# RMS norms of a hybrid decoder step: last squares summed by TensorE, and 1/rms spread as a stationary operand

## Chip, core and metric
One core of one Trainium2 chip runs the kernel. The metric is the time of one execution on the device, in microseconds (us). Three executions of the kernel before gave 2889.6, 2897.57 and 2901.08 us; the median is 2897.57.

## The reference, cut to what matters
One inference step of a decoder with two layers, for a prompt of 1024 tokens and 8 sample tokens. Five RMS norms lie on the way: one ahead of each mixer, one ahead of each MLP, one at the end.

```
def _rmsnorm(x, g):
    y = x * rsqrt(mean(x * x, axis=-1, keepdims=True) + 1e-6)
    return y * g
# layer 0 and layer 1:
h = _rmsnorm(x, norm_mix[layer]);  x = x + mixer(h) ...
h = _rmsnorm(x, norm_mlp[layer]);  x = x + square(relu(h @ w_up)) @ w_down
out = _rmsnorm(x, norm_final)
```

Everything is float32. The kernel splits each float32 operand of the large products into two parts (`h` and `l`, tiles `xh`/`xl`, `uh`/`ul`, `ih`/`il`, `wh`/`wl`) and multiplies three times; the products inside the norm are plain float32 products.

## The kernel before, in words
**Layout.** Activations stand transposed: 1024 features in 8 chunks (`KC`) of 128 partitions, tokens along the free axis. The tokens are cut in two halves, `u = 0` with 512 tokens and `u = 1` with 520 (512 and the 8 samples). `half()` is the output projection and MLP of one layer and one half; the attention and recurrence stages run beside it.

**The norm.** The gain of the norm is multiplied into the split activations before a projection (`gain`), and the factor 1/rms of a token is multiplied into the projection's result. So the projections need not wait for the norm, but the first eviction of their results from PSUM does. The factor is made in four steps:

1. `sumsq` (lines 251 to 262) is called once for each feature chunk `n`. ScalarE squares the chunk (L257 for the first, L260 for the others), VectorE adds the square to the running sum `sq` (L261). In `finish`, the last stage, the same is written out (L1608, L1611, L1612, tiles `fsq` and `fst`).
2. `rms` (lines 264 to 287) adds the 128 partitions: for each 128 tokens (`c`) one product with the 128x128 piece of `sq` as stationary operand and a column of ones as moving operand (L271), which puts the sums of 128 tokens on 128 partitions, one column for each `c`.
3. VectorE divides by 1024 and adds epsilon (L274, L276), GpSimd takes the power -0.5 (L279), into `v` (tile `rv`), which it has set to 1.0 before (L273).
4. The factor is spread over all partitions: for each `c`, VectorE multiplies the identity with a column of `v` (L284, the diagonal `rd`, two buffers), TensorE multiplies it with a full matrix of ones as stationary operand (L285), and ScalarE copies the result to `rb` (L287).

**The eleven calls of rms.** By their row sums on TensorE they lie in the profiled execution at: 1 and 2, the first norm, both halves, at 35 and 39 us (4 and 5 products of 128 tokens); 3, MLP of layer 0, first half, 501 (4); 4, mixer of layer 1, first half, 1050 (4); 5, MLP of layer 0, second half, 1261 (5); 6, mixer of layer 1, second half, 1697 (5); 7, MLP of layer 1, first half, 1929 (4); 8, final norm, first half, 2442 (4); 9, MLP of layer 1, second half, 2512 (5); 10 and 11, final norm, second half, in two blocks of 256 and 264 tokens, at 2870 and 2882 (2 and 3). These are 45 products at L271 and 45 at L285.

**Order.** The program text gives instructions a priority and a queue; a scheduler with a simulated timeline then fixes the order of each engine's queue, among what is ready at that simulated time. Engines work their queues in order. The waits for buffers come from pools of tiles: a tile of a tag with `bufs` buffers waits until the tile that had the buffer has been read for the last time. `half()` is a generator whose pieces are put between the attention stages as filler work for TensorE (`tick`, `fill`); calls 3, 5 and 7 lie in such stretches. Call 8 has no filler left: the second half of layer 1 can begin only after its stage has ended.

**Weights.** `wsplit` loads a block of weights, ScalarE makes `wh` (L117) and GpSimd makes `wl` (L118); GpSimd's queue holds these and the norm's power and memsets.

Of the kernel before, what the change touches and what calls it, by code (L numbers as in the profile page):

```python
# [10 lines left out]
F32 = mybir.dt.float32  # L11
# [3 lines left out]
AF = mybir.ActivationFunctionType  # L15
ALU = mybir.AluOpType
# [6 lines left out]
HW = (NP // 2, T - NP // 2)  # L23
HS = (slice(0, HW[0]), slice(HW[0], T))
PW = (512, 640)
BLOCKS = (((0, 512),), ((0, 256), (256, 264)))
KC = D // 128
# [37 lines left out]
class Step:  # L65
# [98 lines left out]
    def project_rms(self, ps, src, evict, rms, us=(0, 1), w=None):  # L164

        h, l = w or self.wsplit(src, KC)
        pts = []
        for u in us:
            for o, n in BLOCKS[u]:
                pts.append((ps.tile([128, 512], F32, name="acc", tag="acc"), u, o, n))  # L170
                self.mm3(pts[-1][0][:, :n], h, l, self.ih[u], self.il[u], range(KC), slice(o, o + n))
        for u in us:
            rms(u)
        for pt, u, o, n in pts:
            evict(pt[:, :n], u, o, n)
# [75 lines left out]
    def sumsq(self, pool, x, n, sq=None, tags=(("sq", 1), ("ld", 2)), first=None):  # L251

        nc = self.nc
        w = x.shape[1]
        if n == 0:
            sq = (first or pool).tile([128, w if first is None else -(-w // 128) * 128], F32, name="sq", tag=tags[0][0], bufs=tags[0][1])
            nc.scalar.activation(sq[:, :w], x, AF.Square)  # L257
        else:
            t = pool.tile([128, w], F32, name="sqt", tag=tags[1][0], bufs=tags[1][1])
            nc.scalar.activation(t[:, :w], x, AF.Square)  # L260
            nc.vector.tensor_tensor(sq[:, :w], sq[:, :w], t[:, :w], op=ALU.add)  # L261
        return sq

    def rms(self, pool, ps, sq, rb, n):

        nc = self.nc
        full, rest = divmod(n, 128)
        cs = [(c, min(128, n - 128 * c)) for c in range(full + (rest > 0))]
        pt = ps.tile([128, 512], F32, name="acc", tag="acc")
        for c, w in cs:  # L270
            nc.tensor.matmul(pt[:w, c:c + 1], lhsT=sq[:, 128 * c:128 * c + w], rhs=self.ones[:, 0:1], start=True, stop=True)  # L271
        v = pool.tile([128, 9], F32, name="rv", tag="rv")
        nc.gpsimd.memset(v[:], 1.0)  # L273
        nc.vector.tensor_scalar(v[:, :full], pt[:, :full], 1.0 / D, EPS, op0=ALU.mult, op1=ALU.add)  # L274
        if rest:
            nc.vector.tensor_scalar(v[:rest, full:full + 1], pt[:rest, full:full + 1], 1.0 / D, EPS, op0=ALU.mult, op1=ALU.add)  # L276
        h = pool.tile([128, 9], F32, name="rp", tag="rp")
        nc.gpsimd.memset(h[:], -0.5)
        nc.gpsimd.tensor_tensor(v[:, :len(cs)], v[:, :len(cs)], h[:, :len(cs)], op=ALU.pow)  # L279
        for g in range(0, len(cs), 4):  # L280
            pt = ps.tile([128, 512], F32, name="acc", tag="acc")
            for c, w in cs[g:g + 4]:
                d = pool.tile([128, 128], F32, name="rd", tag="rd", bufs=2)
                nc.vector.tensor_scalar(d[:, :w], self.ident[:, :w], v[:, c:c + 1], None, op0=ALU.mult)  # L284
                nc.tensor.matmul(pt[:, 128 * (c - g):128 * (c - g) + w], lhsT=self.ones[:], rhs=d[:, :w], start=True, stop=True)  # L285
            w = min(512, n - 128 * g)
            nc.scalar.copy(rb[:, 128 * g:128 * g + w], pt[:, :w])  # L287

# [20 lines left out]
    def hgrn_gates(self, ph, ps, pr, first, sq):  # L309

        nc, I = self.nc, self.I
        self.fS, self.gS = ([self.dr.tile([4, 128, HW[u]], F32, name=f"{n}{u}") for u in range(2)] for n in ("fS", "gS"))
        lbp = self.col[:, C_LB:C_LB + 12].rearrange("p (h j) -> p h j", j=3)
        lb = self.cp.tile([128, 4], F32, name="lb")
        oml = self.cp.tile([128, 4], F32, name="oml")
        e = ph.tile([128, 4, 3], F32, name="lbe", tag="lbe")
        s = ph.tile([128, 4], F32, name="lbs", tag="lbs")
        nc.vector.tensor_reduce(s[:], lbp, axis=AX.X, op=ALU.max)
        nc.vector.tensor_tensor(e[:], lbp, s[:].unsqueeze(2).to_broadcast([128, 4, 3]), op=ALU.subtract)
        nc.scalar.activation(e[:], e[:], AF.Exp)  # L320
        nc.vector.tensor_reduce(s[:], e[:], axis=AX.X, op=ALU.add)
        nc.vector.reciprocal(s[:], s[:])
        nc.vector.tensor_tensor(lb[:], e[:, :, 0], s[:], op=ALU.mult)
        nc.vector.tensor_scalar(oml[:], lb[:], -1.0, 1.0, op0=ALU.mult, op1=ALU.add)
        for h in range(4):
            z = ph.tile([128, T], F32, name="z", tag="z", bufs=2)
            ev = self.scaled(z, (0, 1))
            if h:
                self.now(self.project(ps, I["w_in_e"][16 + h], ev))
            else:  # L330
                self.project_rms(ps, None, ev, lambda u: self.rms(ph, pr, sq[:, HS[u]], self.rb[u], HW[u]), w=first)
            g = ph.tile([128, T], F32, name="sg", tag="z2", bufs=2)
            nc.scalar.activation(g[:], z[:], AF.Sigmoid)
            nc.vector.tensor_scalar(g[:], g[:], oml[:, h:h + 1], lb[:, h:h + 1], op0=ALU.mult, op1=ALU.add)
            for u in range(2):
                nc.sync.dma_start(self.fS[u][h], g[:, HS[u]])
        for h in range(4):
            z = ph.tile([128, T], F32, name="z", tag="z", bufs=2)
            self.now(self.project(ps, I["w_in_e"][24 + h], self.scaled(z, (0, 1))))
            g = ph.tile([128, T], F32, name="sg", tag="z2", bufs=2)  # L340
            last = nc.scalar.activation(g[:], z[:], AF.Sigmoid)
            nc.gpsimd.tensor_tensor(g[:], g[:], z[:], op=ALU.mult)
            for u in range(2):
                nc.sync.dma_start(self.gS[u][h], g[:, HS[u]])

        self.zero = self.cp.tile([128, 1], F32, name="zero")
        nc.vector.tensor_scalar(self.zero[:], g[:, 0:1], 0.0, 0.0, op0=ALU.min, op1=ALU.max)
        self.ln_exp(last)
# [1151 lines left out]
    def half(self, layer, u, ps, pr, tp=None):  # L1500
# [40 lines left out]
        if not alone:  # L1541
            yield 1
            rms()
# [48 lines left out]
    def finish(self, mp, ps, pr, u, xs, uh, ul, wd):  # L1592

        nc, I, O = self.nc, self.I, self.O
        for n in range(2, 4):
            wd.append(self.down_parts(mp, n))
        rb = self.rb[u]
        for i, (o, m) in enumerate(BLOCKS[u]):
            sl = slice(o, o + m)
            sq = mp.tile([128, 512], F32, name="fsq", tag="t", bufs=2)  # L1600
            for n in range(KC):
                pt = ps.tile([128, 512], F32, name="acc", tag="acc")
                h, l = (w[:, 4 * (n % 2):4 * (n % 2) + 4, :] for w in wd[n // 2])
                self.mm3(pt[:, :m], h, l, uh, ul, range(4), sl)
                x = xs[n][:, sl]
                nc.vector.tensor_tensor(x, pt[:, :m], x, op=ALU.add)  # L1606
                if n == 0:
                    nc.scalar.activation(sq[:, :m], x, AF.Square)  # L1608
                else:
                    t = mp.tile([128, 512], F32, name="fst", tag="u", bufs=2)  # L1610
                    nc.scalar.activation(t[:, :m], x, AF.Square)  # L1611
                    nc.vector.tensor_tensor(sq[:, :m], sq[:, :m], t[:, :m], op=ALU.add)  # L1612
            with self.tc.high_priority():
                self.rms(mp, pr, sq, rb[:, sl], m)
            last = i == len(BLOCKS[u]) - 1
            for n in range(KC):
                x = xs[n][:, sl]
                g = self.col[:, C_FIN + n:C_FIN + n + 1]
                if n % 3 == 1 if last else n % 2:
                    nc.scalar.activation(x, x, AF.Copy, scale=g)  # L1620
                    nc.gpsimd.tensor_tensor(x, x, rb[:, sl], op=ALU.mult)
                else:
                    nc.vector.scalar_tensor_tensor(x, x, g, rb[:, sl], op0=ALU.mult, op1=ALU.mult)  # L1623
                nc.sync.dma_start(O["y"][:, n, HS[u].start + o:HS[u].start + o + m], x)
# [280 lines left out]
```

## Time and profile before

| | before |
|---|---|
| time, median of 3 | 2897.57 us |
| the profiled execution's own time | 2897.19 us |
| its span, first to last instruction | 2895.4 us |
| TensorE matmul (PE) busy | 2748.0 us, 95%, 17404 instructions |
| TensorE weight load (PEld) busy | 2449.9 us, 85% |
| VectorE (DVE) busy | 1377.6 us, 48% |
| GpSimd (POOL) busy | 1142.3 us, 39% |
| ScalarE (ACT) busy | 1038.9 us, 36% |
| mean granted TensorE clock | 0.973 of full speed |

PE and PEld are the two parts of TensorE: a weight load overlaps with the matmul before it. L12 is line 12 of the kernel. In a row of the timeline the text in square brackets is the time that the engine was idle ahead of it, and what ended that. Busy times of matmuls include a modelled end, so the spacing of a run of them says more than the length of one. SP issues the DMAs.

### The profile page before, as it was taken

How to read it: one execution, taken by the hardware profiler on the slowest of the kernel's cores; microseconds unless marked ns; L12 is line 12 of the kernel's file. 1: busy time of each engine (PE TensorE's matmuls, PEld its weight loads, DVE VectorE, ACT ScalarE, POOL GpSimd, SP SyncE). 2: the span in 40 equal slices, each digit the busy share in tenths (PEclk: the TensorE clock that was granted, in tenths of full speed). 3: DMA queues.
4: the chain of work that ended last, by engine and by line, in shares of the span. 5: the costliest groups of instructions: out<-in, count | busy, mean ns of one | idle time of the engine just before them, and what ended most of it. 6: DMA issues, size and time to landing. Idle time of an engine off the chain costs nothing. (4 is left out here: it accounts for less than half of the span.)

```text
span 2895.4 us, 44560 instructions
## 1 busy us (share of the span) xinstructions
PE 2748.0 (95%) x17404; PEld 2449.9 (85%) x17406; DVE 1377.6 (48%) x2666; ACT 1038.9 (36%) x1741; POOL 1142.3 (39%) x689
## 2 busy tenths in 40 slices
PE   8999997989989999999999989989999998999998
PEld 6999886777878878889999979968877776999997
DVE  5134378666664363474322255366544434523234
ACT  4111365552222232463232332155543222423233
POOL 2323323323764434423334435743323343344443
PEclk9999998999999999999999999999999998999999
DMA  4332454224545444423322244643235333322222
GB/s 143 107 125 75 152 163 127 89 83 154 159 115 164 132 163 147 154 88 104 121 95 88 91 158 147 222 128 93 77 110 163 110 107 126 110 89 95 90 94 74
DMA packets 174684, 349.72 MB, mean 121 GB/s; under 512 B 28914, under 2 KB 67298, under 8 KB 174474
## 3 DMA queue, kind: packets, MB, share of 16 engines
q1 hardware_dynamic: 174250, 346.81, 37.0%
q8 instruction: 137, 2.24, 0.3%
q0 software_dynamic: 224, 0.07, 0.2%
q14 instruction: 73, 0.60, 0.1%
HBM read 297.92 MB, written 48.88 MB: 120 GB/s over the span
## 5 line engine op out<-in xcount | busy, mean ns | idle before, releaser
L118 POOL TENSOR_TENSOR wl<-wr,wh 128x1024 fp32r<-128x1024 f32 (+1 forms) x361 | 866.2, 2400 | 1336.0 <-ACT wh L117 1293.1
L117 ACT ACTIVATE wh<-wr 128x1024 fp32r<-128x1024 f32 (+1 forms) x361 | 381.7, 1058 | 1088.1 <-PE acc L151 875.0
L151 PE MATMUL acc<-xh,wh 128*128 128x264 f32 (+2 forms) x2208 | 715.0, 325 | 18.1 <-DVE x L1522 8.0
L151 PE MATMUL acc<-xl,wh 128*128 128x264 f32 (+2 forms) x2208 | 711.3, 323 | 3.1 <-DVE xl L249 3.1
L151 PE MATMUL acc<-xh,wl 128*128 128x264 f32 (+2 forms) x2208 | 709.9, 322 | 0.0
L151 PE MATMUL acc<-uh,wh 128*128 128x512 f32 (+2 forms) x1856 | 607.4, 331 | 21.7 <-DVE x L1522 13.2
L151 PE MATMUL acc<-ul,wh 128*128 128x512 f32 (+2 forms) x1856 | 599.6, 324 | 6.9 <-DVE ul L1489 5.6
L151 PE MATMUL acc<-uh,wl 128*128 128x512 f32 (+2 forms) x1856 | 597.6, 323 | 0.0
L151 PEld LDWEIGHTS acc<-xh,wh 128*128 128x128 f32 x2208 | 420.3, 191 | 51.5 <-issue 10.5
L151 PEld LDWEIGHTS acc<-xl,wh 128*128 128x128 f32 x2208 | 420.7, 191 | 35.6 <-DVE xl L249 4.3
L151 PEld LDWEIGHTS acc<-xh,wl 128*128 128x128 f32 x2208 | 420.0, 190 | 29.4 <-issue 1.2
L1522 DVE TENSOR_TENSOR x<-acc,x 128x256 f32<-128x256 f32 (+1 forms) x464 | 238.3, 517 | 379.0 <-PE acc L151 376.9
L151 PEld LDWEIGHTS acc<-uh,wh 128*128 128x128 f32 x1856 | 353.0, 192 | 56.7 <-DVE x L1522 17.0
L151 PEld LDWEIGHTS acc<-ul,wh 128*128 128x128 f32 x1856 | 354.2, 191 | 33.6 <-DVE ul L1489 7.6
L151 PEld LDWEIGHTS acc<-uh,wl 128*128 128x128 f32 x1856 | 353.8, 191 | 26.8 <-issue 0.4
L1495 DVE SCALAR_TENSOR_TENSOR acc<-acc,rb 128x256 f32<-128x256 f32 (+2 forms) x192 | 100.2, 524 | 242.4 <-PE acc L151 237.7
L151 PE MATMUL acc<-ih,wh 128*128 128x512 f32 (+3 forms) x600 | 193.0, 322 | 7.3 <-ACT wh L117 4.7
L151 PE MATMUL acc<-ih,wl 128*128 128x512 f32 (+3 forms) x600 | 192.2, 323 | 6.5 <-POOL wl L118 6.5
L151 PE MATMUL acc<-il,wh 128*128 128x512 f32 (+3 forms) x600 | 192.2, 321 | 0.0
L225 DVE TENSOR_TENSOR z<-acc,rb 128x512 f32<-128x512 f32 (+2 forms) x138 | 69.6, 511 | 231.2 <-PE acc L151 216.6
L1498 DVE TENSOR_TENSOR ul<-acc,uh 128x256 fp32r<-128x256 f32 (+2 forms) x192 | 98.5, 513 | 135.6 <-ACT uh L1497 134.9
L151 PEld LDWEIGHTS acc<-ih,wh 128*128 128x128 f32 (+1 forms) x600 | 113.8, 190 | 16.8 <-ACT wh L117 6.7
(409 smaller groups left out, 3406.1 us busy)
## 6 DMA issues: line engine op xcount, KB each, us to landing
wr<-in_w_up SPq DMA_DIRECT2D x128, 512.0 KB
wr<-in_w_down SPq DMA_DIRECT2D x128, 512.0 KB
wr<-in_w_in_o SPq DMA_DIRECT2D x48, 512.0 KB
wr<-in_w_out SPq DMA_DIRECT2D x32, 512.0 KB
wr<-in_w_in_e SPq DMA_DIRECT2D x27, 512.0 KB
qd<-qS SPq DMA_DIRECT2D x64, 128.0 KB
dk<-in_cache_k_a SPq DMA_DIRECT2D x32, 256.0 KB
dk<-in_cache_v_a SPq DMA_DIRECT2D x32, 256.0 KB
```

Source lines behind the costliest of these rows:

```text
L117: nc.scalar.activation(h[:, :kk, :m], r[:, :kk, :m], AF.Copy)
L118: nc.gpsimd.tensor_tensor(l[:, :kk, :m], r[:, :kk, :m], raw(h[:, :kk, :m]), op=ALU.subtract)
L151: nc.tensor.matmul(out, lhsT=w[:, k, :m], rhs=a[:, sl], start=(n == 0), stop=(n == last))
L225: nc.vector.tensor_tensor(d, p, r, op=ALU.mult)
L1495: nc.vector.scalar_tensor_tensor(p, p, 0.0, self.rb[u][:, sl], op0=ALU.max, op1=ALU.mult)
L1498: nc.vector.tensor_tensor(L[:, sl], p, raw(H[:, sl]), op=ALU.subtract)
L1522: nc.vector.tensor_tensor(x[f][:, sl], pt[:, :m], x[f][:, sl], op=ALU.add)
```

## The change
In `sumsq` the square of the last chunk is no longer added by VectorE; it is handed on beside the running sum, as a pair. `rms` multiplies both members of the pair with the column of ones and accumulates the two products in PSUM (so the first has `start`, the second `stop`). `hgrn_gates` passes the pair with a token offset `t0` instead of slices. For the sums that `odd_gates` uses (calls 4 and 6), which live in another pool, there are now two tiles `sq0` and `sq7` instead of one tile `sq`. In `finish` the eighth add is left out likewise.

For the spreading, the diagonal `rd` and its VectorE instruction go. The stationary operand is now the column of `v`, repeated 128 times along the free axis by its access pattern, and the moving operand is the identity.

```
     def sumsq(self, pool, x, n, sq=None, tags=(("sq", 1), ("ld", 2)), first=None):
-        if n == 0:
-            sq = (first or pool).tile([128, w if first is None else -(-w // 128) * 128], F32, name="sq", tag=tags[0][0], bufs=tags[0][1])
-            nc.scalar.activation(sq[:, :w], x, AF.Square)
-        else:
-            t = pool.tile([128, w], F32, name="sqt", tag=tags[1][0], bufs=tags[1][1])
+        if n in (0, KC - 1):
+            if first is None:
+                tag, bufs = tags[n > 0]
+                t = pool.tile([128, w], F32, name="sqt" if n else "sq", tag=tag, bufs=bufs)
+            else:
+                t = first.tile([128, -(-w // 128) * 128], F32, name="sq", tag=f"sq{n}")
             nc.scalar.activation(t[:, :w], x, AF.Square)
-            nc.vector.tensor_tensor(sq[:, :w], sq[:, :w], t[:, :w], op=ALU.add)
+            return (sq, t) if n else t
+        t = pool.tile([128, w], F32, name="sqt", tag=tags[1][0], bufs=tags[1][1])
+        nc.scalar.activation(t[:, :w], x, AF.Square)
+        nc.vector.tensor_tensor(sq[:, :w], sq[:, :w], t[:, :w], op=ALU.add)
         return sq
     def rms(...):
         for c, w in cs:
-            nc.tensor.matmul(pt[:w, c:c + 1], lhsT=sq[:, 128 * c:128 * c + w], rhs=self.ones[:, 0:1], start=True, stop=True)
+            for i, s in enumerate(sq):
+                nc.tensor.matmul(pt[:w, c:c + 1], lhsT=s[:, t0 + 128 * c:t0 + 128 * c + w], rhs=self.ones[:, 0:1], start=(i == 0), stop=(i == 1))
...
-                d = pool.tile([128, 128], F32, name="rd", tag="rd", bufs=2)
-                nc.vector.tensor_scalar(d[:, :w], self.ident[:, :w], v[:, c:c + 1], None, op0=ALU.mult)
-                nc.tensor.matmul(pt[:, 128 * (c - g):128 * (c - g) + w], lhsT=self.ones[:], rhs=d[:, :w], start=True, stop=True)
+                nc.tensor.matmul(pt[:, 128 * (c - g):128 * (c - g) + w], lhsT=v[:, c:c + 1].to_broadcast([128, 128]), rhs=self.ident[:, :w], start=True, stop=True)
     def finish(...):
-                    nc.vector.tensor_tensor(sq[:, :m], sq[:, :m], t[:, :m], op=ALU.add)
+                    if n < KC - 1:
+                        nc.vector.tensor_tensor(sq[:, :m], sq[:, :m], t[:, :m], op=ALU.add)
-                self.rms(mp, pr, sq, rb[:, sl], m)
+                self.rms(mp, pr, (sq, t), rb[:, sl], m)
```

## Rows read from the trace of the kernel before

**Rows 1.** The page's first part: busy us, share of span, instructions of each engine.
```profile
PE 2748.0 (95%) x17404; PEld 2449.9 (85%) x17406; DVE 1377.6 (48%) x2666; ACT 1038.9 (36%) x1741; POOL 1142.3 (39%) x689
```

**Rows 2.** Waits of PE: waiting line, what ended it, us in total, times, longest.
```profile
PE acc L271 <- DVE sq L261: 12.1, 5, 4.5
...
PE acc L285 <- DVE rd L284: 5.3, 3, 1.8
...
PE acc L271 <- DVE fsq L1612: 3.6, 1, 3.6
```

**Rows 3.** Line 271: count, duration ns min/median/max, first and last start us, forms.
```profile
L271 PE MATMUL acc<-ones,sq x80: 163/250/373, 35.4 to 2512.6; 128*128 128x1 f32 x72, 128*8 128x1 f32 x8
...
L271 PE MATMUL acc<-ones,fsq x10: 163/250/353, 2870.0 to 2883.1; 128*128 128x1 f32 x8, 128*8 128x1 f32 x2
```

**Rows 4.** Stretches: length, busy us of PE, PEld, DVE, ACT, POOL, then PEclk, DMA, GB/s.
```profile
1691.00:1710.00 19.00, 13.68 (x56) 10.53 (x55) 10.12 (x19) 7.28 (x13) 4.66 (x9) 0.73 0.80 260
...
2438.00:2466.00 28.00, 15.43 (x83) 14.01 (x82) 13.26 (x22) 4.71 (x8) 3.38 (x2) 0.70 0.63 219
```

**Rows 5.** Timeline at calls 1 and 2: start us, busy us, engine, line, instructions, idle before.
```profile
39.07 1.07 PE L271 MATMUL acc<-ones,sq 128*128 128x1 f32 x10
...
42.59 0.80 PE L285 MATMUL acc<-rd,ones 128*128 128x128 f32 x2 [1.80 <-DVE rd L284]
...
43.42 0.58 ACT L287 COPY rb<-acc 128x512 f32<-128x512 f32 x1 [3.39 <-PE acc L285]
...
44.04 1.29 DVE L225 TENSOR_TENSOR z<-acc,rb 128x512 f32<-128x512 f32 x2 [1.51 <-ACT rb L287]
...
44.78 0.79 PE L151 MATMUL acc<-xh,wh 128*128 128x512 f32 x1 [1.40 <-DVE z L225]
```

**Rows 6.** Timeline at calls 3, 5, 6 and 7.
```profile
501.02 1.87 PE L271 MATMUL acc<-ones,sq 128*128 128x1 f32 x8 [0.36 <-DVE sq L261]
...
1260.63 2.00 PE L271 MATMUL acc<-ones,sq 128*128 128x1 f32 x10 [1.13 <-DVE sq L261]
...
1693.76 0.62 ACT L260 ACTIVATE sqt<-x 128x520 f32<-128x520 f32 x1
...
1696.64 1.96 PE L271 MATMUL acc<-ones,sq 128*128 128x1 f32 x10 [4.49 <-DVE sq L261]
...
1928.44 0.68 DVE L653 TENSOR_TENSOR Pl<-pm,Ph 128x512 fp32r<-128x512 f32 x1
...
1928.57 1.05 PE L271 MATMUL acc<-ones,sq 128*128 128x1 f32 x8 [2.14 <-DVE sq L261]
```

**Rows 7.** Timeline at call 8.
```profile
2439.52 0.63 ACT L260 ACTIVATE sqt<-x 128x512 f32<-128x512 f32 x1 [0.34 <-DVE x L1522]
2440.18 1.96 DVE L261 TENSOR_TENSOR sq<-sq,sqt 128x512 f32<-128x512 f32 x1 [0.76 <-ACT sqt L260]
...
2442.20 1.87 PE L271 MATMUL acc<-ones,sq 128*128 128x1 f32 x8 [3.94 <-DVE sq L261]
...
2445.41 0.48 DVE L284 TENSOR_SCALAR rd<-ident,rv 128x128 f32<-128x128 f32 x2 [1.15 <-POOL rv L279]
...
2445.76 2.40 PE L285 MATMUL acc<-rd,ones 128*128 128x128 f32 x8 [1.69 <-DVE rd L284]
```

**Rows 8.** Timeline at call 11.
```profile
2881.15 0.42 ACT L1611 ACTIVATE fst<-x 128x264 f32<-128x264 f32 x1 [1.10 <-DVE x L1606]
...
2882.18 1.11 PE L271 MATMUL acc<-ones,fsq 128*128 128x1 f32 x6 [3.57 <-DVE fsq L1612]
...
2884.64 0.48 DVE L284 TENSOR_SCALAR rd<-ident,rv 128x128 f32<-128x128 f32 x2 [1.03 <-POOL rv L279]
...
2885.07 1.68 PE L285 MATMUL acc<-rd,ones 128*128 128x128 f32 x6 [1.78 <-DVE rd L284]
```

**Rows 9.** Line 284, columns as in rows 3.
```profile
L284 DVE TENSOR_SCALAR rd<-ident,rv x45: 205/283/2391, 38.1 to 2885.9; 128x128 f32<-128x128 f32 x40, 128x8 f32<-128x8 f32 x5
```

**Rows 10.** The page's costliest groups, GpSimd's casts: count, busy us, mean ns, idle before.
```profile
L118 POOL TENSOR_TENSOR wl<-wr,wh 128x1024 fp32r<-128x1024 f32 (+1 forms) x361 | 866.2, 2400 | 1336.0 <-ACT wh L117 1293.1
```

More of the change, by code (lines that the diff above doesn't have):

```diff
@@ L254, in sumsq, with rms @@
         w = x.shape[1]
-        if n == 0:
-            sq = (first or pool).tile([128, w if first is None else -(-w // 128) * 128], F32, name="sq", tag=tags[0][0], bufs=tags[0][1])
-            nc.scalar.activation(sq[:, :w], x, AF.Square)
-        else:
-            t = pool.tile([128, w], F32, name="sqt", tag=tags[1][0], bufs=tags[1][1])
+        if n in (0, KC - 1):
[4 more added lines that the diff above has]
+                t = first.tile([128, -(-w // 128) * 128], F32, name="sq", tag=f"sq{n}")
             nc.scalar.activation(t[:, :w], x, AF.Square)
-            nc.vector.tensor_tensor(sq[:, :w], sq[:, :w], t[:, :w], op=ALU.add)
+            return (sq, t) if n else t
+        t = pool.tile([128, w], F32, name="sqt", tag=tags[1][0], bufs=tags[1][1])
+        nc.scalar.activation(t[:, :w], x, AF.Square)
+        nc.vector.tensor_tensor(sq[:, :w], sq[:, :w], t[:, :w], op=ALU.add)
         return sq
-    def rms(self, pool, ps, sq, rb, n):
+    def rms(self, pool, ps, sq, rb, n, t0=0):
         nc = self.nc
@@ L330, in hgrn_gates @@
             else:
-                self.project_rms(ps, None, ev, lambda u: self.rms(ph, pr, sq[:, HS[u]], self.rb[u], HW[u]), w=first)
+                self.project_rms(ps, None, ev, lambda u: self.rms(ph, pr, sq, self.rb[u], HW[u], HS[u].start), w=first)
             g = ph.tile([128, T], F32, name="sg", tag="z2", bufs=2)
```

## The prediction, made before the changed kernel ran
> **The bound.** I read the busy table first: TensorE is busy 2748.0 of the 2895.4 us, every other engine less than half [rows 1]. So time is lost or won only where TensorE waits, or where it gets more to do. Next the list of waits, for TensorE alone: at the row-sum products (L271) it waits 12.1 us in five waits for the running sum and 3.6 us once in `finish`, at the spreading products (L285) 5.3 us in three waits for a diagonal [rows 2]. The reader is to see that the stretches in question hold about 21 us of 2895: the most that can be taken out of these waits is 0.7%. The third view is the group of L271: 80 + 10 pairs of weight load and matmul for 45 products, two pairs each [rows 3]; I call a pair a pass. Last the timeline at each of the eleven `rms` calls, in the order of front's list, with the granted clock around them: 0.73 and 0.70 of full speed in two 19 to 28 us stretches with a call in them [rows 4]. TensorE has waited there, and the passes that follow run at 1.2 GHz.
>
> **Added products.** Term 1, +13.9 us. Each of the 45 row-sum products becomes two accumulating ones, so 90 passes come on, on the engine that bounds. Their price is set by the stretch. In call 2, with no wait ahead, ten passes took 1.07 us, 0.107 each [rows 5]. In calls 3, 5, 6, 8 and 11 they took 1.87/8 = 0.23, 2.00/10 = 0.20, 1.96/10 = 0.20, 1.87/8 = 0.23 and 1.11/6 = 0.19 [rows 6, 7, 8], about twice as much: the lower clock. Calls 1, 2, 4, 7, 9 and 10 get 8+10+8+8+10+4 = 48 passes, 5.1 us; the five slow calls get 8+10+10+8+6 = 42, at their own prices 1.84+2.00+2.00+1.84+1.14 = 8.8 us. I take the rows of each call because the same instruction will run in the same place; ends: 9.6 us (all at 0.107) and 20.7 us (all at 0.23).
> The Trainium skill (TensorE: Matmul & The Clock Gate, "LDWEIGHTS (loading the stationary operand)") lets a load take its columns over 1.2 GHz, 107 ns for 128, with no word on the gated clock; by that all 90 passes would cost 9.6 us and the forecast would be 4.3 us lower. The passes of 0.107 us agree with it, those of 0.19 to 0.23 do not, and they decide.
>
> **Removed adds.** Term 2, -8.3 us. Ten adds go. What counts is how far L271 moves forward, which is bounded by TensorE's wait ahead of it and by what is late next, the last square on ScalarE. Call 3: it waited 0.36 us, all goes. Call 5: 1.13, all goes, since the last square was done 3 us earlier. Call 6: it began at 1696.64, the square ended at 1693.76 + 0.62 = 1694.38; 2.26 us. Call 7: 2.14 us waited, but afterwards TensorE needs `Pl`, which VectorE makes behind the add from 1928.44 on, in 0.68 us; the add is of the same kind and size, so without it `Pl` is ready at about 1928.44. 16 passes from 1926.43 end at 1928.15, then 0.3 us of new wait: 1.85 [rows 6]. Call 8: the square ended at 2440.15, the add took 1.96 us (GpSimd's cast ran beside it) and L271 began at 2442.20: 2.05 us [rows 7]. Call 9: nothing taken, as TensorE works until just before. Call 11: the square ended at 2881.57, L271 began at 2882.18: 0.6 us [rows 8]. Sum 0.36+1.13+2.26+1.85+2.05+0.6 = 8.3. In calls 1, 4 and 10 TensorE had other products until after the add: nothing. The ends are 0 (TensorE finds itself waiting for something else) and the 15.7 us of the waits' list.
> The last square now lives on until L271 has read it. Its buffer is next asked for by squares or loads much later in each stage, so no wait comes of that; in `finish` the second block's third square takes it over, and starts after the products of the first block. The second padded tile for `odd_gates` takes 2 to 2.5 KB per partition of its pool; I cost it at nothing.
>
> **Removed diagonals.** Term 3, -5.3 us. 45 VectorE instructions go, median 0.283 us [rows 9]. They have two buffers, so the third waits for TensorE's products of the first, and TensorE for it. Call 1: TensorE waited 1.80 us for a diagonal, then 1.40 us for `z`, which needs the copied `rb`. The projections ahead end two passes before 39.07, at 38.86; with 8 more passes for call 1's sums, 8 spreading ones and 20 for call 2's sums, TensorE is through at 38.86 + 36 x 0.107 = 42.7, and copy and `z` have fallen beside the 20. If the spreading products stay behind call 2's sums, copy (0.58) and `z` (1.29 / 2 = 0.65) follow: 43.9. The next projection began at 44.78; the 18 new passes (1.9 us) are already in term 1, so the gain to be set down is 2.8 to 4.0, 3.4 in the middle [rows 5]. Call 8: 0.35 us from the diagonal's start to the product, and eight passes took 2.40 where 8 x 0.23 = 1.87 would do: 0.9 us, and the whole of it counts, as the copy of `rb` and all that follows stand behind it [rows 7]. Call 11: 0.43 us and 1.68 - 6 x 0.19 = 0.54, together 1.0 us, at the very end [rows 8]. In the other calls the products lie scattered between other TensorE work. Ends: 2 us (calls 8 and 11 alone) and 8 us.
> GpSimd's memset of the next `rv` waited for the last diagonal; it now waits for the last spreading product, which stands later in the chain. Behind it are weight casts. In call 1 the last spreading product would be over at 38.86 + 16 x 0.107 = 40.6 us at best, where the last diagonal ended at about 42.59, and at 42.7 at worst; so no cast is late by more than a pass [rows 5]. Elsewhere I cost it at nothing, because the old diagonals waited for the same products.
>
> **Small terms.** -2.5 us. VectorE loses 45 diagonals and ten adds, some 20 us of work spread over eleven places where TensorE also waits for its other results; between 0 and -4, I take -1.5, about two adds' worth. Where TensorE waits less, its clock may stay up: 0.27 of 19 us is 5.1 us in one such stretch [rows 4]; between 0 and -5, I take -1.
>
> **Sum.** 13.9 - 8.3 - 5.3 - 2.5 = -2.2 us on the profiled execution's own 2897.19 us (span 2895.4, 1.8 us around it), which is 0.4 us off the median 2897.57. Forecast: 2895 us. A measurement of this kernel tells a change from none at about 0.5%, 14.5 us, so this is no change.
>
> **Rivals.**
> *The passes are paid and not repaid (slower).* Place: calls 3, 5, 6 and 7, where TensorE stands between attention work. If the order that the planner writes puts another waiting product ahead of L271, or L285 right behind the power on GpSimd, whose queue holds casts of 2.4 us [rows 10], the wait merely changes its name. Price: term 1 whole, of terms 2 and 3 only calls 1, 8 and 11 (3.4+2.05+0.9+0.6+1.0 = 8.0): +6 us; with three new waits of a cast's length, 7 us, +13: 2903 to 2910 us. It decides once the starts of calls 3, 5, 6 and 7 (5.6 us together) move by less than 3 us. For it: nothing but the planner holds those places. Against: in six waits at L271 the add itself is named as what ended them [rows 2].
> *The order and the clock settle better (faster).* All instructions are placed by simulated times, so shorter `rms` chains move everything after them. With the 42 slow passes at 0.107 (-4), clock kept up in two stretches (-5) and one wait of a few microseconds gone: about -13, 2884 us. For it: the low clock at five calls; against: an order can as well get worse.
> *The spread operand loads slowly.* The stationary operand of L285 becomes one column read 128 times; no row shows such a load. Bounds: 0.107 us a pass, as for the full tile, and 0.32 if it were three times that; 90 x 0.21 = +19 us, 2914 us. I take the lower bound: the passes of L271 and L285 are alike for different operands. The Trainium skill (the same page, "Weight-path perf modes") says that fast weight load is not used for FP32 operands, so an unusual step has nothing to switch off; no run here shows it yet.
>
> **Chances.** Forecast 0.60, not repaid 0.16, better order 0.19, slow load 0.05. The range reaches from 2880 (better order with its spread) to 2911 (not repaid); the slow load and the tails are left out. Faster than 2883.1: half of better order and a twelfth of the forecast, 0.15. Slower than 2912.1: the slow load, a tenth of not repaid and a twentieth of the forecast, 0.09. The rest, 0.76, within 0.5%.
>
> **What would show it.** In the profile after: L271 with 180 pairs, TensorE's busy time some 10 to 14 us up; no wait of L271 for `sq`, shorter waits for the square on ScalarE; L285 with 90 loads as long as those of L271, its passes next to each other; the copy of `rb` in call 8 about 1 us sooner behind the last square. I am wrong if L285's loads are longer, if L271 still waits as long for something else, or if stretches without any `rms` call change their length by more than the eleven together.

## The result, and the profile after

| | before | after |
|---|---|---|
| time, median of 11 runs each | 2893.78 us (2887.18 to 2901.08) | 2877.05 us (2866.99 to 2883.62) |
| ratio, 95% interval | | 0.9941 [0.9925, 0.9957] |
| profiled span, mean granted clock | 2895.4 us, 0.973 | 2881.8 us, 0.975 |

The change takes 0.6% off, 16.7 us; a second timing beside the later experiments gave 0.9940 [0.9919, 0.9960]. The forecast was 2895 us, no change. The time is inside the range of 2880 to 2911 in neither timing; it lies at the place of the rival "the order and the clock settle better" (2884), and 7 us beyond it.

The busy table of the changed kernel, columns as in [rows 1]:

```profile
PE 2751.9 (95%) x17494; PEld 2456.8 (85%) x17496; DVE 1355.8 (47%) x2611; ACT 1037.6 (36%) x1741; POOL 1142.8 (40%) x689
```

TensorE has 90 matmul records more and is busy 3.9 us longer, not the 10 to 14 that I had written down. Its waits at the norm (columns as in [rows 2]; L276 are the row sums now, L288 the spreading):

```profile
PE acc L276 <- DVE sq L265: 6.2, 4, 3.2
...
PE acc L288 <- POOL rv L284: 3.1, 3, 1.4
...
PE acc L276 <- ACT sq L261: 2.2, 2, 1.4
...
PE acc L276 <- DVE fsq L1616: 1.6, 1, 1.6
...
PE acc L276 <- ACT sqt L261: 0.9, 1, 0.9
...
PE acc L276 <- ACT fst L1614: 0.4, 1, 0.4
```

Together 14.4 us, where before had 21.0 [rows 2]. That is 6.6 us; the change brought 16.7. So most of the gain does not stand in the list of waits of these two lines. One sign that I had named did not come: L276 still waits for `sq`, 6.2 us in four waits, now for the add of the seventh square. The groups (columns as in [rows 3]):

```profile
L276 PE MATMUL acc<-ones,sq x98: 163/250/373, 34.2 to 2501.1; 128*128 128x1 f32 x88, 128*8 128x1 f32 x10
...
L288 PEld LDWEIGHTS acc<-ident,rv x90: 185/191/338, 39.5 to 2872.3; 128*128 128x128 f32 x90
```

and the same loads before:

```profile
L285 PEld LDWEIGHTS acc<-rd,ones x90: 186/192/338, 38.7 to 2886.3; 128*128 128x128 f32 x90
```

98 matmuls here, with 62, 10 and 10 of the other tiles, make the 180 that were forecast. A column read 128 times loads in a median of 191 ns, the full tile of ones in 192: "the spread operand loads slowly" did not happen.

**Where the time went.** Starts shift, so I cut every profile at the same weight casts of GpSimd (the n-th L118) and compared the stages between them. Four profiles have the calls of `rms` as before (before, the same again, and two experiments below that touch other things), four have them as after. The first four are before, r1, n1 and g2, the others after, r3, g1 and f1. Times name the stage in the first profile of before; the forecast of a call is its share of terms 1 to 3.

| stage (calls) | four as before, us | four as after, us | mean difference | forecast |
|---|---|---|---|---|
| 0-84 (1, 2) | 81.8 to 84.1 | 76.7 to 79.0 | -4.3 | -1.5 |
| 482-562 (3) | 80.1 to 80.5 | 72.9 to 74.0 | -6.8 | +1.5 |
| 1027-1087 (4) | 59.3 to 60.1 | 60.2 to 60.8 | +0.6 | +0.9 |
| 1235-1357 (5) | 122.6 to 124.0 | 118.5 to 123.3 | -2.4 | +0.9 |
| 1693-1738 (6) | 44.3 to 45.6 | 44.3 to 44.6 | -0.5 | -0.3 |
| 1893-1963 (7) | 69.5 to 69.7 | 65.1 to 67.1 | -3.5 | -1.0 |
| 2434-2490 (8) | 56.0 to 56.2 | 52.9 to 53.5 | -2.9 | -1.1 |
| 2490-2563 (9) | 71.5 to 73.1 | 71.8 to 73.3 | +0.2 | +1.1 |
| 2835-end (10, 11) | 59.7 to 60.3 | 59.3 to 59.6 | -0.7 | 0.0 |
| all stages without a call | | | +4.0 | small terms, -2.5 |

Sum -16.3 us. Four stages carry it: calls 1 and 2, 3, 7 and 8, -17.5 together. In each of them the four profiles of one kind do not overlap with the other four. Calls 5 and 6 do overlap; what call 5 wins, the stage behind it gives back (+1.6).

The same eight profiles, over the whole span and in the mean of four each, split the -16.3 us once more. TensorE is idle 21.5 us less (145.6 to 124.1) and busy 5.3 us more (2743.7 to 2749.0). From start to start, waits left out, the 90 row-sum passes of before took 12.9 us and the 180 of after 24.5: the added ones cost 11.7 us, 0.13 each. So the rest of TensorE's work took some 6 us less, and the time at the lower clock level (1.2 GHz) fell from 146 to 132 us.

**Calls 1 and 2.** Two stretches of before (columns as in [rows 4]):

```profile
35.00:50.00 15.00, 11.80 (x66) 10.21 (x66) 4.75 (x11) 1.64 (x2) 7.44 (x10) 0.77 0.27 74
50.00:66.00 16.00, 15.26 (x95) 13.55 (x94) 5.81 (x13) 6.09 (x7) 2.68 (x2) 1.00 0.23 80
```

and of after:

```profile
35.00:50.00 15.00, 15.00 (x110) 13.99 (x110) 1.67 (x5) 1.95 (x3) 6.95 (x9) 1.00 0.27 74
50.00:66.00 16.00, 16.00 (x114) 15.02 (x113) 7.00 (x12) 5.69 (x7) 2.90 (x3) 1.00 0.39 135
```

3.9 us in which TensorE stood are gone (3.20 + 0.74), and so is the low clock: 0.77 over 15 us is 6.9 us at 1.2 GHz; TensorE was busy for 4.9 of them, which cost half of that, 2.5 us. With the 18 added passes (1.9 us) that makes -4.5; the table's mean is -4.3, these two profiles differ by 5.4 at 84 us. The granted clock of 0.77 came back in every profile with calls 1 and 2 as before, and the full clock in every one with them as after, but for the one with doubled passes (e7, 0.89). There the clock fell for 3.4 us at 37 us although TensorE had not waited since 21.7 us; ahead of the fall it had made 24 row-sum passes in a row. So a wait is not the only thing behind which the clock fell. How TensorE's standing in before comes about is in its timeline, behind [rows 5]'s first row:

```profile
40.11 2.34 POOL L118 TENSOR_TENSOR wl<-wr,wh 128x1024 fp32r<-128x1024 f32 x1 [1.87 <-ACT wh L117]
...
40.60 1.93 DVE L284 TENSOR_SCALAR rd<-ident,rv 128x128 f32<-128x128 f32 x1 [1.04 <-PE acc L285]
```

One diagonal takes 1.93 us, where the median is 0.283 [rows 9]: it ends when GpSimd's cast does. TensorE then waits 1.80 us for it, and 1.40 us for `z` [rows 5]. After:

```profile
39.63 1.05 PE L288 MATMUL acc<-ident,rv 128*128 128x128 f32 x8
...
40.72 0.58 ACT L290 COPY rb<-acc 128x512 f32<-128x512 f32 x1
...
41.34 1.29 DVE L225 TENSOR_TENSOR z<-acc,rb 128x512 f32<-128x512 f32 x2 [4.97 <-ACT rb L290]
```

The eight spreading passes follow the projections without a wait, copy and `z` lie beside call 2's sums.

**Call 8**, the timeline of after:

```profile
2430.04 0.38 PE L276 MATMUL acc<-ones,sq 128*128 128x1 f32 x2 [0.61 <-DVE sq L265]
...
2430.68 0.63 ACT L261 ACTIVATE sqt<-x 128x512 f32<-128x512 f32 x1 [0.34 <-DVE x L1525]
...
2431.36 0.38 PE L276 MATMUL acc<-ones,sqt 128*128 128x1 f32 x2 [0.94 <-ACT sqt L261]
...
2433.12 0.16 DVE L279 TENSOR_SCALAR rv<-acc 128x4 f32<-128x4 f32 x1 [2.54 <-PE acc L276]
...
2434.45 1.80 PE L288 MATMUL acc<-ident,rv 128*128 128x128 f32 x8 [1.37 <-POOL rv L284]
2436.30 0.58 ACT L290 COPY rb<-acc 128x512 f32<-128x512 f32 x1 [4.99 <-PE acc L288]
```

From the end of the last square to the copy of `rb`: 2436.30 - 2431.31 = 4.99 us; before, with the copy at 2448.19, 2448.19 - 2440.15 = 8.04 [rows 7]. The reader is to see two things. The single wait of 3.94 us [rows 7] has become two of 0.61 and 0.94, with two passes between them. And the 14 passes behind the square take 1.7 us, 0.12 each, where eight took 1.87 before. The clock of the two kernels in these sums, after first:

```profile
2429.00:2434.40 5.40, 2.53 (x18) 1.94 (x17) 1.45 (x3) 1.95 (x3) 3.38 (x2) 1.00 0.29 93
```

```profile
2441.80:2446.00 4.20, 2.11 (x9) 2.03 (x10) 0.99 (x4) 0.00 (x0) 1.04 (x1) 0.50 0.38 125
```

In these two profiles the sums run at 2.4 GHz behind the short waits, and at 1.2 behind the long one. The kernels do not fix that. The second profile of before (r1) has the same wait and its eight passes at the full clock, since the low clock began only after them; its stage is as long (55.96 us, 56.07 in the first):

```profile
2438.12 1.05 PE L271 MATMUL acc<-ones,sq 128*128 128x1 f32 x8 [3.94 <-DVE sq L261]
```

In the second profile of after (r3) the last four sums ran at the low clock. And the spreading passes are slow in both kernels: in after eight took 1.80 us, 0.225 each, in this stretch:

```profile
2434.40:2440.00 5.60, 3.48 (x14) 2.88 (x14) 3.08 (x5) 1.65 (x3) 0.00 (x0) 0.53 0.48 180
```

Over four profiles each, the low clock holds for 17.1 us of this stage before and for 14.5 us after. It is shorter, not gone. TensorE's idle time there falls by 3.3 us, and that carries the -2.9.

### The profile page after: what moved, and what is told of

The parts are those of the page before. It is cut to its first block, busy times and chain, and to the rows that moved or that the text cites. A ratio compares the mean times of both kernels' runs of the same rounds, so it can differ in the third digit from the quotient of the medians.

```text
span 2881.8 us, 44697 instructions
## 1 busy us (share of the span) xinstructions
PE 2751.9 (95%) x17494; PEld 2456.8 (85%) x17496; DVE 1355.8 (47%) x2611; ACT 1037.6 (36%) x1741; POOL 1142.8 (40%) x689
## 3 DMA queue, kind: packets, MB, share of 16 engines
q8 instruction: 138, 2.26, 0.3%
## 5 line engine op out<-in xcount | busy, mean ns | idle before, releaser
L118 POOL TENSOR_TENSOR wl<-wr,wh 128x1024 fp32r<-128x1024 f32 (+1 forms) x361 | 866.7, 2401 | 1341.9 <-ACT wh L117 1292.9
L151 PE MATMUL acc<-uh,wh 128*128 128x512 f32 (+2 forms) x1856 | 605.8, 330 | 21.7 <-DVE x L1525 10.8
L1498 DVE SCALAR_TENSOR_TENSOR acc<-acc,rb 128x256 f32<-128x256 f32 (+1 forms) x192 | 100.2, 523 | 248.8 <-PE acc L151 241.5
L225 DVE TENSOR_TENSOR z<-acc,rb 128x512 f32<-128x512 f32 (+2 forms) x138 | 69.7, 511 | 253.9 <-PE acc L151 228.1
L1501 DVE TENSOR_TENSOR ul<-acc,uh 128x256 fp32r<-128x256 f32 (+1 forms) x192 | 98.2, 513 | 140.6 <-ACT uh L1500 140.4
```

Of the source, the lines that this page charges most:

```text
L118: nc.gpsimd.tensor_tensor(l[:, :kk, :m], r[:, :kk, :m], raw(h[:, :kk, :m]), op=ALU.subtract)
L151: nc.tensor.matmul(out, lhsT=w[:, k, :m], rhs=a[:, sl], start=(n == 0), stop=(n == last))
L225: nc.vector.tensor_tensor(d, p, r, op=ALU.mult)
L1498: nc.vector.scalar_tensor_tensor(p, p, 0.0, self.rb[u][:, sl], op0=ALU.max, op1=ALU.mult)
L1501: nc.vector.tensor_tensor(L[:, sl], p, raw(H[:, sl]), op=ALU.subtract)
```

## The experiments

Each was timed beside runs of the kernel before; intervals are 95%. The first group splits the change.

**e1, spreading alone.** Before, with `L284` and `L285` replaced by the changed line:

```
-                d = pool.tile([128, 128], F32, name="rd", tag="rd", bufs=2)
-                nc.vector.tensor_scalar(d[:, :w], self.ident[:, :w], v[:, c:c + 1], None, op0=ALU.mult)
-                nc.tensor.matmul(pt[...], lhsT=self.ones[:], rhs=d[:, :w], start=True, stop=True)
+                nc.tensor.matmul(pt[...], lhsT=v[:, c:c + 1].to_broadcast([128, 128]), rhs=self.ident[:, :w], start=True, stop=True)
```

> Only the spreading is changed (no diagonals, column of v as stationary operand); the last adds stay and no passes are added. Theory A (diagonals and the waits and low clock behind them make the gain; the added passes cost about what the earlier row sums give back): 14 to 20 us faster than the kernel before, ratio 0.993 to 0.995, with calls 1 and 2 shortened by about 7 us (the 5.4 seen plus 1.9 us of passes that are not there). Rival B (the removed adds make the gain by letting the row sums start earlier): only the 5 us of my third term, ratio 0.998. Rival C (the order that the planner writes makes the gain): stretches at calls 3, 7, 8 and 9 come out differently from the changed kernel's, total anywhere between -20 and +10 us.

Measured 0.9961 [0.9944, 0.9978], 2877.02 us. Calls 1 and 2 came as theory A had them (7.1 us shorter); the ratio lies between A's and B's.

**e2, last squares alone.** The pair and the accumulating product as in the change, but calls 4 and 6 keep the add (72 added passes), and the diagonals stay.

> Only the last squares go to TensorE (calls 4 and 6 keep their add, since their second tile does not fit beside the diagonals, so 72 passes are added instead of 90); diagonals stay. Theory A: no gain, ratio 0.999 to 1.002 (-3 to +6 us), calls 1 and 2 longer by 1 to 2 us. Rival B: 8 to 12 us faster, ratio 0.996 to 0.997, with call 3 about 6 us shorter. Rival C: no prediction for single calls.

Measured 1.0002 [0.9985, 1.0019]. In its profile the stages of calls 7 and 8 are 2.3 and 2.2 us shorter than the mean of before. That of calls 1 and 2 is 3.2 shorter, where theory A had 1 to 2 us more: no diagonal takes over 0.29 us there, and 35 to 50 us run at full clock. But the profiled execution (2881.55 us) is the third fastest of 12, whose median is that of before. So the removed adds alone bring nothing that can be measured in the time; where the rest gives those microseconds back is not shown.

**e3, four diagonals.** `bufs=2` becomes `bufs=2 if pool is self.M else 4` for `rd`: more buffers in calls 1, 2, 4, 6, 10 and 11, nothing else.

> The kernel before with four buffers instead of two for the diagonals in calls 1, 2, 4, 6, 10 and 11 (two stay in calls 3, 5, 7, 8, 9), nothing else. If what delays calls 1 and 2 is the coupling by two buffers (third diagonal waits for the first product), calls 1 and 2 shorten by 3 to 5 us and the whole by as much, ratio 0.998 to 0.999. If it is the diagonals' own time on VectorE beside GpSimd's cast (1.93 us for one), they shorten by less than 1.5 us. By rival C the rest of the kernel moves by several us although nothing in it is changed but the order.

Measured 0.9981 [0.9964, 0.9997]. The stage of calls 1 and 2 is 5.6 us shorter, nearly as much as with the new spreading (e1 7.1, e4 6.8). No diagonal of calls 1 and 2 takes over 0.29 us here either, so e3 takes away the held diagonal together with the waits for a buffer.

**e4, spreading in calls 1 and 2 alone** (a flag of `rms`, set in `hgrn_gates`).

> The kernel before with the new spreading in calls 1 and 2 alone. Theory A: -7 us in the first 84 us, and about the same, -5 to -9 us, at the end, ratio 0.997 to 0.998. Rival B: -3.4 us at most in the first 84 us. Rival C: the gain at the start is lost or doubled later at calls whose text is as before (the order around calls 3, 5 and 7 does change).

Measured 0.9955 [0.9937, 0.9974], 2875.40 us: as much as the whole change, and more than theory A had.

**e5, all but calls 1 and 2.** The changed kernel, in which `sumsq` adds the last square and `rms` makes diagonals when they are called for the first norm.

> The changed kernel, but calls 1 and 2 as before the change (the last squares added on VectorE, diagonals with two buffers); calls 3 to 11 changed. Theory A (nearly all of the gain is in calls 1 and 2, where VectorE's diagonals made TensorE wait and the clock fell behind the wait; in the other calls the passes cost what the waits give back): ratio to before 0.998 to 1.002, the stretch from 35 to 50 us at a granted clock near 0.77 again. Rival B (the waits of calls 3, 5 to 8 and 11 carry the gain): 0.994 to 0.997. Rival C (the planner's order of the rest): the time is then not foretold by which calls are changed, and no stage that holds a changed call is shorter by more than its waits.

Measured 0.9976 [0.9958, 0.9994], 35 to 50 us at 0.77 again. Between the two theories' numbers: calls 7 and 8 keep their 3.1 and 3.2 us, so theory A, which put nearly all into calls 1 and 2, is too narrow. And the stage of call 3, with call 3 changed, is 80.95 us: 0.7 us longer than before, not 6.8 shorter.

**f3, diagonals of calls 1 and 2 on ScalarE**, still two buffers:

```
+                if act:
+                    nc.scalar.activation(d[:, :w], self.ident[:, :w], AF.Copy, scale=v[:, c:c + 1])
```

> The kernel before with the diagonals of calls 1 and 2 made by ScalarE (a copy with a scale per partition) instead of VectorE; still two buffers, no added passes, everything else as before. Theory A1 (the dear part of call 1 is the diagonal on VectorE that takes 1.93 us while GpSimd casts for 2.34 us): no diagonal over 0.6 us, 84 us reached 3 to 7 us sooner than before, ratio 0.9955 to 0.9985. Rival A2 (the two buffers and the trip from product to diagonal are dear, on whatever engine): 35 to 50 us still near 0.77 and 84 us reached within 2 us of before, ratio 0.999 to 1.002.

Measured 0.9997 [0.9980, 1.0013]. Its stretch, and e3's behind it:

```profile
35.00:50.00 15.00, 13.36 (x77) 11.65 (x77) 1.41 (x4) 4.42 (x10) 5.27 (x9) 0.89 0.28 75
```

```profile
35.00:50.00 15.00, 13.60 (x94) 12.38 (x93) 4.30 (x16) 2.23 (x3) 5.84 (x10) 1.00 0.29 76
```

Off VectorE, 1.6 of the 3.2 us of standing go and half of the low clock; with four buffers 1.8 us go and all of the low clock. 84 us is reached 3.1 us sooner than the mean of before, within A1's 3 to 7, but A1's ratio was missed; A2's ratio came, its clock and its 2 us did not. So of the 7.1 us that the new spreading takes off this stage (e1), about 3 go without the held diagonal, and the others only when the trips between product and diagonal become fewer (e3) or none. That split is worked out from single profiles.

**x1, calls 1 and 2 alone, in both parts.** Calls 3 to 11 keep adds and diagonals.

> The kernel before with only calls 1 and 2 changed, in both parts (last squares to TensorE, new spreading); calls 3 to 11 keep adds and diagonals. Theory A (the planner's order behind calls 1 and 2 makes the gain at call 3; the order written around call 3 is nearer the changed kernel's than any other): 84 us reached 4.5 to 6 us sooner, the stage 482 to 562 us 5 to 7 us shorter although call 3 is as before, ratio to before 0.994 to 0.997. Rival (call 3's own edit): that stage within 1.5 us of before's 80.3 us, ratio 0.997 to 0.999.

Measured 0.9965 [0.9942, 0.9989]. The stage of call 3 took 72.79 us, 7.4 less than before's mean, with call 3 not touched. 84 us was reached 4.1 us sooner, a little under the 4.5 expected. The waits of TensorE in that stage that differ (`Pl`, L653, is the low part of the attention weights, `x`, L1522, the residual sum; both come from VectorE), in before:

```profile
PE po L679 <- DVE Pl L653: 6.5, 2, 5.3
...
PE acc L151 <- DVE x L1522: 2.8, 1, 2.8
```

in e5, which changes call 3 but not 1 and 2:

```profile
PE acc L278 <- DVE sq L267: 4.3, 1, 4.3
PE acc L151 <- DVE x L1532: 2.9, 1, 2.9
PE po L689 <- DVE Pl L663: 1.6, 1, 1.6
```

and in after, then in x1:

```profile
PE po L682 <- DVE Pl L656: 1.9, 2, 1.6
PE acc L276 <- DVE sq L265: 1.9, 1, 1.9
```

```profile
PE po L685 <- DVE Pl L659: 1.6, 1, 1.6
```

After and x1 have no wait for `x` there and only short ones for `Pl`; e5 has a short one for `Pl`, but a long one for `sq` and that for `x`. The order of TensorE's products in the stage is the same, up to a record or two, in before, r1, n1, g2 and f3, and another in after and x1: the planner has moved them. As far as the runs show, that takes calls 1 and 2 changed in both parts; call 3's own edit is not needed (x1) and does not bring it alone (e5). With the new spreading alone in calls 1 and 2 (e4) the stage takes 78.2 us.

**e7, last squares twice.** The changed kernel, the product of the last squares made twice against a column of 0.5 (45 products, 90 passes more, same sum):

```
-            for i, s in enumerate(sq):
+            for i, (s, o) in enumerate(((sq[0], self.ones[:, 0:1]), (sq[1], self.col5[:]), (sq[1], self.col5[:]))):
```

> The changed kernel with the product of the last squares made twice, each against a column of 0.5 instead of 1: 45 more products, 90 more passes, the same sum. Theory A (an added pass costs TensorE its own time, since TensorE is the bound): 90 x 0.107 = 9.6 us up to 90 x 0.23 = 20.7 us more than the changed kernel, ratio to before 0.997 to 1.002, the busy time of TensorE 8 to 12 us above the changed kernel's. Rival B (the passes fall into the waits ahead of the calls): the changed kernel's time within 3 us, ratio 0.993 to 0.996.

Measured 0.9981 [0.9961, 1.0001], 2882.52 us beside 2873.06 of the changed kernel: 9.5 us for 90 passes by the medians, 11.7 by the means, each to within some 4 us. That is 0.1 to 0.13 us a pass. Its busy row says +11.7 against the first profile of after:

```profile
PE 2763.6 (96%) x17584; PEld 2467.0 (86%) x17586; DVE 1344.9 (47%) x2611; ACT 1038.0 (36%) x1741; POOL 1145.4 (40%) x690
```

A pass costs its own time, in the mean nearer to that at the upper clock level than at the lower.

**n1, r1, r3: what is not the change.** n1 is before with a memset of 128x8 on GpSimd in each call; r1 and r3 are before and after, profiled again.

> The kernel before with one more memset of 128x8 on GpSimd in each call of rms (some 0.1 us each, 11 in all), read by nobody. Theory A (what is gained lies in calls 1 and 2, and other stages of the experiments differ by when VectorE's queue meets GpSimd's): the norm itself takes what it takes before, 35 to 50 us at a granted clock near 0.77, ratio 0.998 to 1.002; if the product of hq and hpe on VectorE at 804 us, which takes 10.30 us there, meets GpSimd otherwise, that stage is 7 us shorter and the ratio 0.9965 to 0.999. Rival C (any edit moves the time by the planner's order): the order of TensorE's queue is the same here, so exactly 1.0 within 0.001.

> The kernel before, unchanged, profiled once more. Theory A: calls 1 and 2 take the same (granted clock of 35 to 50 us near 0.77, 66 us reached within 2 us of the first profile); the stage from 801 to 847 us, which holds no call and was 7 us shorter in four experiments, is a matter of the execution and may be 7 us shorter here too. Rival C: that stage stays as long as in the first profile of before, within 1 us.

> The changed kernel, unchanged, timed beside the others and profiled once more. Theory A: ratio 0.992 to 0.996, 35 to 50 us at full clock again, 84 us reached 5 to 8 us before the kernel of before; the stages without a call may differ from the first profile of it by up to 7 us each. Rival C: each stage within 1 us of the first profile.

n1: 1.0012 [0.9997, 1.0027], slower by a hair, if at all. r1 (one execution) 2891.5 us, r3 0.9940 [0.9919, 0.9960]; their stages are in the table above. The stage from 801 to 847 us, which holds no call, took 45 to 46 us in both profiles of before and of after, and 38 to 40 us in n1 and every experiment but f1 (44.7). What stands there in before:

```profile
803.91 3.77 POOL L863 TENSOR_TENSOR dk<-dk,dq 128x512 f32<-128x512 f32 x3
...
804.29 10.30 DVE L404 TENSOR_TENSOR hq<-hq,hpe 128x256 f32<-128x256 f32 x1
...
807.63 2.39 POOL L118 TENSOR_TENSOR wl<-wr,wh 128x1024 fp32r<-128x1024 f32 x1
...
809.98 1.27 POOL L863 TENSOR_TENSOR dk<-dk,dq 128x512 f32<-128x512 f32 x1
...
811.22 0.66 POOL L405 TENSOR_TENSOR hk<-hk,hpe 128x256 f32<-128x256 f32 x1
...
811.84 2.47 POOL L863 TENSOR_TENSOR dk<-dk,dq 128x512 f32<-128x512 f32 x2
...
817.34 0.77 PE L151 MATMUL acc<-xh,wh 128*128 128x512 f32 x1 [7.38 <-DVE x L1522]
```

A product of VectorE (two tiles of the recurrence), 0.67 us in the median of its 48, stands until GpSimd's eight instructions are through; the addition behind it is late, and TensorE stands for 7.38 us. In r1, after and r3 such a product takes 11.7 to 11.8 us; in n1 none is long, yet the ratio is not the 0.9965 to 0.999 that theory A had for that. Three experiments made one such product on GpSimd instead. In f1, the kernel after with one word changed at L407, it is that of head 1, level 6:

```
-            nc.vector.tensor_tensor(Q[:, :, hh:], ...)
+            (nc.gpsimd if (u, h, li) == (1, 1, 6) else nc.vector).tensor_tensor(Q[:, :, hh:], ...)
```

> The changed kernel, with one product of hq and hpe (second half, head 1, last level), which VectorE held for 11.71 us at 793 us, made by GpSimd instead. Theory A (VectorE's product stood until GpSimd's queue had a gap, the additions behind it were late, and TensorE stood for 8.45 us and then ran at half clock): the stage of 801 to 847 us is 6 to 8 us shorter, time 4 to 9 us under the changed kernel, ratio to before 0.990 to 0.9935. Rival (the wait is a matter of the stage's load on GpSimd and comes back at the next product): no shorter, ratio 0.9935 to 0.997.

f1 moved another product than the one that stands, which took 10.0 us again. 0.9924 [0.9902, 0.9945], the lowest median of all (2867.73 us), but not told apart from the changed kernel. With the right one, (1, 2, 2), in the kernel after (g1) and before (g2):

> The changed kernel with the product of hq and hpe that stood for 11.71 us (second half, head 2, level 2) made by GpSimd instead of VectorE. Theory A: VectorE's additions are no longer behind it, TensorE's wait of 8.45 us in 801 to 847 us falls to under 4 us and that stage is 6 to 8 us shorter; time 3 to 8 us under the changed kernel, ratio to before 0.9905 to 0.9935. Rival (the next product or another one meets the same queue): a product of over 9 us elsewhere, and the ratio as for the changed kernel, 0.993 to 0.996.

> The kernel before with the same product moved to GpSimd. Theory A: that stage 6 to 8 us shorter than in the first profile of before, ratio to before 0.9965 to 0.999 (less than the stage, since before reaches the short form of it in some executions too). Rival: ratio 0.999 to 1.002, the wait comes back elsewhere.

The long product is gone from both, and TensorE's longest wait in that stage falls to 3.25 and 3.28 us, so theory A was right on the stage; yet the ratios are 0.9946 [0.9926, 0.9967] and 1.0007 [0.9992, 1.0023]. g1's stage shrinks by 5.5 us and g2's by 7.0 against the first profile of before, and 1.8 and 2.7 us are given back by 976 us. So A was wrong on the time: over 6 and 12 executions the 7 us do not show. Why not stays open; that executions of one kernel differ in this stage would explain it, but two profiles of each kernel don't prove it.

**f4, a mixture.** New spreading everywhere; calls 1, 2, 4 and 6 keep their add.

> The changed spreading in all calls; the last squares go to TensorE only in calls 3, 5, 7, 8, 9, 10 and 11 (MLP and final norms), calls 1, 2, 4 and 6 keep the add on VectorE: 27 added products instead of 45, so 36 passes fewer than the changed kernel. Theory A (a pass costs 0.107 us and calls 1, 2, 4 and 6 get nothing back for it): 36 x 0.107 = 3.9 us less than the changed kernel, ratio to before 0.991 to 0.995. Rival (planner's order and meetings of VectorE and GpSimd are larger than that): anything from 0.990 to 0.998, with stages without a call carrying the difference.

0.9953 [0.9936, 0.9970], 2875.02 us: the 36 passes saved don't show. Its stage of calls 1 and 2 is 6.8 us shorter than before, that of call 3 only 1.2, and that of call 8, with the edit of after, 0.2 longer. Its waits at the norm are those of after; but the low clock holds for 20.5 us there (13.7 in after), and TensorE waits 2.19 us for `uh` behind the norm (1.16 in after). So a longer low clock and one other wait undo the gain of this stage. No version beat the changed kernel by more than the intervals.

## Why the prediction was wrong

**What held.** TensorE is the bound; a pass costs its time (e7). The 90 added passes cost 11.7 us, where term 1 had 13.9. Term 3 in call 1 is near, 3.4 forecast and 3.9 of standing gone. Terms 2 and 3 of call 8 are right: 2.39 us less wait ahead of the sums (3.94 against 0.61 + 0.94), 2.05 forecast. L288 loads as forecast, and the passes of call 8 are next to each other. Outside call 3 the idle time of TensorE fell by 14.3 us, where terms 2 and 3 and the help to VectorE had 14.7. That the sum is so close is in part luck: call 6 gave 0.9 of its 2.26 us, and call 4 1.3 where I had none.

**The first step that failed: the clock, in the small terms.** I gave it -1 us, within 0 and -5. The rest of TensorE's work took some 6 us less, and 14 us of low clock are gone, which at half speed are worth up to 7: 5.1 each in the stages of calls 1 and 2 and of call 3, 3.4 in that of call 7, 2.6 in that of call 8. In calls 1 and 2 alone it is 2.5 us: I counted a gain of 3.4 us for the wait and nothing for the 6.9 us at 1.2 GHz in and behind it. My rows gave the granted clock around calls 6 and 8 only; that of 35 to 50 us, 0.77, was not among them.

Term 1 used the same clock the wrong way. It took the price of a pass from "the rows of each call because the same instruction will run in the same place", 0.19 to 0.23 us in five calls. The place did not hold. In call 8 the passes cost 0.6 us more than before, where I charged 1.84. In call 3 they stayed at 0.2 us each. In call 4, at 0.09 us a pass before, they now stand behind a new wait:

```profile
1030.24 0.35 PE L276 MATMUL acc<-ones,sq 128*128 128x1 f32 x2 [3.18 <-DVE sq L265]
...
1032.03 3.15 PE L276 MATMUL acc<-ones,sq 128*128 128x1 f32 x14 [0.86 <-ACT sq L261]
```

They cost 2.5 us there instead of 0.86. These errors nearly cancel, which is luck; 2.2 us too much are left.

**The second, and larger: the order was costed at nothing.** -6.8 us at call 3, where I had +1.5; 7.2 us of idle time are gone there, where I had 0.36. x1 shows that call 3's edit is not the cause, and e5 that without calls 1 and 2 it gives +0.7, not far from the forecast. This is the mechanism of the rival "better order", "one wait of a few microseconds gone", to which I gave 0.19. It can be had the other way too: e1 and e3 are 7.0 and 4.7 us longer than before between 562 and 802 us, where neither edits anything. The order at call 3 (6.8), the clock (some 5) and the passes (2.2) make up the 14 us between -2.2 and -16.3. Why the low clock falls where it does is left open; r1 and r3 show that it moves between executions of one kernel.

**What the split says of the design.** Moving the adds brings nothing by itself (e2), the new spreading nearly all (e1), and of it the share in calls 1 and 2 as much as the whole (e4). Why e4, with 6.8 us in its own stage, is 13.5 us faster in the medians is shown only in part: its two stages from 84 to 562 us are 4.4 us shorter too, with no edit in them.

**The rivals.** "Not repaid": no; the stages of calls 7 and 8 became shorter by more than their passes cost, that of call 5 no longer. "Slow load": no. "Better order and clock": yes, with a larger share of clock than I priced. Of the signs of being wrong, none came: stages without a call changed by +4.0 us, the eleven calls together by -20.3.

## What to carry to other kernels

A pass that is slow behind a wait has no fixed price: it cost 0.11 us at full clock and 0.2 at the low one, and which of them it met changed with the order and from execution to execution. Over all calls the added passes came to 0.13 us each, between the two. When a wait goes, add to it half of the time that the engine is busy at the low clock behind it, read from the granted clock of that very stretch in more than one profile. Where a scheduler writes the order, no stage's length is safe from an edit elsewhere; forecast with a spread of one order change (here 5 to 7 us) either way, and compare stages over several profiles before naming a cause. A ping-pong between TensorE and VectorE with two small buffers costs more than its instructions, and a constant as moving operand can remove it.

## What the runs showed of the hardware

VectorE's instructions between SBUF tiles can stand while GpSimd works: 1.93 us for a diagonal of 0.283 beside a cast, 10.30 us for a product of 0.67 through eight GpSimd instructions back to back (11.71 us in after), ending when GpSimd's queue had a gap, while its reductions and its additions from PSUM ran at their 0.68 us beside GpSimd. The Trainium skill (SBUF — State Buffer, "Who interferes with whom") says that a VectorE instruction with two SBUF inputs contends with a GpSimd instruction that reads SBUF, and that the port pair they share is an exclusive lock. The trace agrees that VectorE's product stands, and shows it standing through eight instructions, not one. Second, a stationary operand with a stride of zero loads as fast as a full tile (191 and 192 ns). Third, the low clock falls in different places in executions of one kernel: in call 8 it began 0.5 us ahead of the sums in the first profile of before and 0.3 us behind them in the second.
